# Expert weights loaded as 4 KB runs per partition, and every sixth chunk of them multiplied whole as fp32

## The chip, the core and the metric

The kernel runs on one core of a Trainium2 chip. The metric is device time in microseconds: the span from the first to the last instruction of one execution and the little that lies around it. The median of three executions of the kernel before is 1588.86 us (1588.35 to 1589.14). One execution was recorded by the hardware profiler; it took 1591.64 us, and its span is 1590.0 us. All rows below are from that one.

## The reference, cut to what matters

The reference is one block with a mixer, a memory attention and a hierarchical mixture of experts, and then two more layers with attention and a feed-forward part, on 256 tokens of width 1024 in float32. The change concerns the experts: 32 of them, each with two matrices of 1024 x 512 and one of 512 x 1024.

```python
N_GROUPS = 4
EXPERTS_PER_GROUP = 8
TOPK_IN_GROUP = 2
D_EXPERT = 512

def hier_moe(h, w_rg, b_rg, w_re, b_re, w_gate, w_up, w_down):
    ...
    # one group per token, two experts in it, softmax weights
    def run_block(args):
        e, tok, w = args
        xb = xt[tok]
        hid = jax.nn.silu(xb @ w_gate[e]) * (xb @ w_up[e])
        return (hid @ w_down[e]) * w[:, None].astype(xb.dtype)
```

## The kernel before

All 32 experts are computed, each on up to 32 of its own tokens (tokens beyond that go through a loop that does not run here unless some expert has more than 32). Two experts make a unit; there are 16 units. For each unit, `up(u)` streams 16 chunks of weights (gate and up matrices) and `down(u - 1)` streams 8 chunks of the unit before. So a unit takes 24 chunks, and the stage 384. A chunk is 256 rows of 512 columns of float32, 512 KB: two tiles of 128 x 512 side by side in an SBUF slot (`KC = 2`). `load` (line 276) issues its transfer on SyncE's queue with the row index split as `(k p)`: partition p gets row p of the first 128 rows and row p of the second 128, two runs of 2 KB. For the down matrices the columns are halved and a chunk has 256 rows of one half. `nextraw` hands out the slots in a ring of about 27 places (tiles named raw, kTc, vc, hBl, hAl, hAh, hBh, gain), SyncE issues in order, and each transfer waits until its slot has been read.

A float32 matrix is multiplied in two halves of fp32r, a short type that TensorE multiplies faster. `high` (line 286) makes the high half on ScalarE, `low` (line 291) makes the rest, raw minus high, on VectorE (7 chunks early in the stage on GpSimd). Each has four buffers. `parts` (line 1010) then issues four products of 128 x 512 for the chunk (line 1015): two on the high half, two on the low half. The stationary operand of 128 columns holds both halves of the tokens' rows (32 tokens x 2 experts x high and low), and `comb` adds them later.

`stream` (line 1021) runs over the chunks: it takes the next loaded chunk, has the halves made, issues the products, and then calls `tick`, which runs what was put on an agenda for this number of chunks (`clock`). So small work is placed between the chunks by `at(n, ...)`: copying the gate and up sums (line 1068), adding the halves of the hidden rows (line 1070), the sigmoid and the products that make them (lines 1078 to 1083), copying the down sums Y (line 1099), adding a pair of units to the residual x by products with Y (the scatter, lines 1106 and 1110), and gathering the tokens' rows for the next two units (`take`, line 933, and `put`, lines 940 and 942). Nearly all of it is kept in program order on each engine. `take` multiplies 128 columns of x, taken contiguously, with a 0/1 selection; it gives 128 rows of the transposed x, in the order in which the chunks have their rows.

The scatter and the gather use plain float32 operands; the trace records each such product as two instructions.

Of the kernel before, what the change touches and what calls it, by code (L numbers as in the profile page):

```python
# [13 lines left out]
F32 = mybir.dt.float32  # L14
# [6 lines left out]
P = 128  # L21
# [3 lines left out]
KD = D // P  # L25
KC = 2
RAW = 4
MOE_RAW = 16
LAG = 3
POOLED = (4, 24, 3)  # L30
EARLY = 25
PAST = 16
OVER = 10
# [81 lines left out]
def forward(ctx: ExitStack, tc: tile.TileContext, a: dict, out: bass.AP):  # L115
    nc = tc.nc
    mm = nc.tensor.matmul
# [3 lines left out]
    wraw = ctx.enter_context(tc.tile_pool(name="wraw", bufs=RAW))  # L121
# [10 lines left out]
    def new(pool, shape, dt=F32, name="t", **kw):  # L132
        return pool.tile(shape, dt, name=name, tag=name, **kw)

    def bcast_rows(ap, n=P):

        return bass.AP(tensor=ap.tensor, offset=ap.offset, ap=[[0, n]] + [list(x) for x in ap.ap])
# [75 lines left out]
    def slices(*halves):  # L213

        return [(h[0][:, k], h[1][:, k]) for h in halves for k in range(h[0].shape[1])]
# [53 lines left out]
    def keep(ins):  # L269
        return tc.keep_in_program_order(ins)  # L270

    def chunk(pool, tag, kc, n, dt=F32):
        v = new(pool, [P, KC, 512], dt, name=tag, **({"bufs": 2} if tag == "Y" else {}))
        return v if n == 512 else v.rearrange("p k n -> p (k n)")[:, 0:kc * n].rearrange("p (k n) -> p k n", n=n)

    def load(parts, kc, n, pool=wraw, tag="raw"):

        raw = chunk(pool, tag, kc, n)
        at = 0
        for src in parts:  # L280
            w = src.shape[1]
            nc.sync.dma_start(out=raw[:, :kc, at:at + w], in_=src.rearrange("(k p) n -> p k n", p=P))
            at += w
        return raw

    def high(raw, kc, n, order=free):
        h = chunk(whi, "wh", kc, n, F32R)
        order(nc.scalar.activation(h[:, :kc], raw[:, :kc], AF.Copy))  # L288
        return h

    def low(raw, h, kc, n, order=free, eng=nc.vector):
        l = chunk(wlo, "wl", kc, n, F32R)
        order(eng.tensor_sub(l[:, :kc], raw[:, :kc], h[:, :kc].bitcast(F32)))  # L293
        return l
# [51 lines left out]
    def add_to_x(xs, W, then=None, loaded=None, order=free):  # L346
        for half in range(2):
            hs = slice(half * 512, (half + 1) * 512)

            def evac(t, ps):  # L350
                nc.vector.tensor_add(x[:, t, hs], x[:, t, hs], ps)
                if then:
                    then(x[:, t, hs], t, half)

            dense(xs, [W[:, hs]], 512, evac, 3 if half else 1, loaded if half else None, order)
# [361 lines left out]
    def nextraw():  # L717

        return next(v for v in raws if not closing or v[0] is not big or v[1] in ("kTc", "vc"))

    wg, wu, wd = a["w_exp_gate"][0], a["w_exp_up"][0], a["w_exp_down"][0]
    ahead, ready = collections.deque(), collections.deque()
# [4 lines left out]
    with tc.tile_pool(name="crossp", bufs=1, reuse_waits="tile") as cp:  # L727
# [4 lines left out]
        for h in range(4):  # L732
            ps = new(psm, [P, NT, T], name="mm")
# [6 lines left out]
            p = pair[:, h % 2]  # L740
# [8 lines left out]
        for h in range(4):  # L749
            p = pm[h]  # L750
# [33 lines left out]
        def feed_moe(src, t, half):  # L784
# [19 lines left out]
        xr = new(rowp, [P, NT, D], name="xr")  # L804
# [5 lines left out]
        nc.gpsimd.dma_start(out=rb[:, 4:36], in_=bcast_rows(a["b_router_expert"][0]))  # L810
        first = []
        add_to_x(slices(oT), a["w_co"][0], feed_moe, lambda: first.extend(
            load([wg[0, k0 * P:(k0 + KC) * P, :]], KC, 512, *nextraw()) for k0 in range(0, KD, KC)))
        ss = new(sml, [P, NT], name="s2")
        nc.vector.tensor_add(ss, ssm[:, 0], ssm[:, 1])
        rm = rstd_of(ss, NT, D, "m")
# [16 lines left out]
    def s3(name, n):  # L833
        return new(mp, [P, NT, n], name=name)
# [53 lines left out]
    UNITS = [(2 * u, 2 * u + 1) for u in range(16)]  # L888
    last = len(UNITS) - 1
    xs2 = []  # L890
    for u in range(2):
        xs2.append(new(mp, [P, KD, 3, 2, 32], F32R, name="xs%d" % u))
        if u == 0:
            wt = s3("wt", 32)
            upcoming = [W[e, k0 * P:(k0 + KC) * P] for i in range(2) for e in UNITS[i] for W in (wg, wu) for k0 in range(0, KD, KC)]
            ahead.extend(load([src], KC, 512, *nextraw()) for src in upcoming[len(first):][:EARLY])
    hs2 = []
    for v in xs2:
        nc.gpsimd.memset(v[:, :, 1].bitcast(F32), 0.0)
# [5 lines left out]
    agenda, clock = collections.defaultdict(list), [0]  # L905

    def at(n, fn, *args):
        if n <= 0:
            fn(*args)
        else:  # L910
            agenda[clock[0] + n].append((fn, args))

    def tick():
        clock[0] += 1
        for fn, args in agenda.pop(clock[0], ()):
            fn(*args)
# [11 lines left out]
    def take(u, k0):  # L928

        ps = new(pst, [P, 4, 2, 2, 32], name="tp")  # L930
        for k in range(4):
            for t in range(NT):
                keep(mm(ps[:, k].rearrange("p u e r -> p (u e r)"), xr[:, t, (k0 + k) * P:(k0 + k + 1) * P],
                        sels[u][:, t].rearrange("p e r -> p (e r)"), start=(t == 0), stop=(t == NT - 1)))
        return ps

# [7 lines left out]
    def gather(u, first, step, lag):  # L944
        select(u)
        for i in range(2):
            at(first + step * i, lambda k0: at(lag, put, k0, take(u, k0)), 4 * i)
# [59 lines left out]
        nc.gpsimd.dma_start(out=wodram, in_=wos)  # L1007
        nc.gpsimd.dma_start(out=iddram.rearrange("(o n) -> o n", o=1), in_=ids)

    def parts(xf, e, nk, last, acc, W, col):  # L1010

        def go(k0, ww):
            for i in range(2):
                for k in range(KC):
                    keep(mm(acc, xf[:, k0 + k, e * 64:e * 64 + P], ww[i][:, k],  # L1015
                            start=(e == 0 and k0 == 0 and i == 0 and k == 0),
                            stop=(e == last and k0 + KC == nk and i == 1 and k == KC - 1)))

        return [(W[k0 * P:(k0 + KC) * P, col:col + 512], functools.partial(go, k0)) for k0 in range(0, nk, KC)]

    def stream(chunks):
        for src, go in chunks:
            if ready:
                go(ready.popleft())
            else:
                raw = ahead.popleft() if ahead else load([src], KC, 512, *nextraw())
                h = high(raw, KC, 512, keep)
                go((h, low(raw, h, KC, 512, keep, nc.gpsimd if clock[0] < POOLED[1] and clock[0] % POOLED[0] == POOLED[2] else nc.vector)))
            tick()

    def flat(v):
        return v.rearrange("p k a b c -> p k (a b c)")
# [21 lines left out]

    def up_chunks(u, G=None, U=None):
        return [c for e, x_ in enumerate(UNITS[u]) for acc, W in ((G, wg), (U, wu))
                for c in parts(flat(xs2[u % 2]), e, KD, len(UNITS[u]) - 1, acc, W[x_], 0)]

    def up(u):

# [26 lines left out]
        at(LAG + 2, hidden)  # L1087

    def down_chunks(u, Y=(None, None)):
        return [c for e, x_ in enumerate(UNITS[u]) for half in range(2)  # L1090
                for c in parts(flat(hs2[u % 2]), e, 4, len(UNITS[u]) - 1, Y[half], wd[x_], half * 512)]

    def down(u):

        Y = [new(psa, [P, 512], name="at") for _ in range(2)]
        stream(down_chunks(u, Y))
        Yg[u] = new(mp, [P, 2, 512], name="Y", bufs=2)
        for half in range(2):
            at(LAG - 2 + 2 * half, lambda *v: keep(nc.scalar.copy(*v)), Yg[u][:, half], Y[half])
# [89 lines left out]
    for u in range(last + 1):  # L1189
        if u == last:  # L1190
            closing.append(True)
        if u == last - 1:

            gf, g12 = xr[:, 0], xr[:, 1]
            nc.gpsimd.dma_start(out=gf[0:1], in_=bcast_rows(a["g_final"], 1))
            nc.gpsimd.dma_start(out=g12[0:1], in_=bcast_rows(a["norm_attn_2"][0], 1))
            nc.gpsimd.tensor_tensor(g12[0:1], g12[0:1], gf[0:1], op=ALU.mult)
            for i, (v, half) in enumerate(itertools.product((gf, g12), range(2))):
                at(GAINS + 2 * i, to_all, v[:, half * 512:half * 512 + 512])
        up(u)  # L1200
        if u == OVER:

            for (src, _), v in zip(down_chunks(u - 1) + up_chunks(u + 1), itertools.takewhile(lambda v: v not in shared, raws)):
                ahead.append(load([src], KC, 512, *v))
            overflow()
        if u % 2 and u < last:
            gather(u + 1, 1, 2, 3)
        if u == last:
            sums.extend([new(psm, [P, 512], name="mm") for _ in range(NT)] for _ in range(2))
            for v, n in zip(both, ADDX):  # L1210
                at(n, add, *v, None)
        if u:
            down(u - 1)
            if u % 2 == 0:
                scatter([u - 2, u - 1], LAG + 2, 3, 2)

    Y = [new(psa, [P, 512], name="at") for _ in range(2)]
# [66 lines left out]
    for t, half in both:  # L1284
        v = x[:, t, hs(half)]
# [268 lines left out]
```

## Time and profile before

| | |
|---|---|
| median of three executions | 1588.86 us |
| profiled execution | 1591.64 us, span 1590.0 us |
| mean granted TensorE clock | 0.989 of 2.4 GHz |
| TensorE busy | 1532.9 us, 96% of the span |
| VectorE busy | 1190.1 us, 75% |
| ScalarE busy | 992.1 us, 62% |
| bytes moved | 383.59 MB, 241 GB/s over the span |

A row of the page's groups gives line, engine, operation, the tiles (out<-in), their shapes, the count, the busy time and the mean of one, then the idle time of the engine just before them and what ended it. Busy time of TensorE holds modelled ends of pipelined products, so the distance between starts tells more than a duration. The slices of the page are 1590.0 / 40 = 39.75 us each; the expert products lie in the eighth to the twenty-first.

### The profile page before, as it was taken

What the parts mean: (1) busy time and instruction counts of PE and PEld (TensorE: products, weight loads), DVE (VectorE), ACT (ScalarE), POOL (GpSimd) and SP (SyncE); (2) the same over time, 40 slices, a digit from 0 to 9 for tenths busy, and PEclk for the clock granted to TensorE, in tenths of its full rate; (3) what the DMA queues carried; (4) which work ended last, traced back from release to release, by engine and by line L of the source; (5) the groups of instructions that cost most, each with busy time, mean ns of one, the idle gap of its engine ahead of it and who ended that gap; (6) DMA issues with size and microseconds to landing.
All of it is one profiled execution on the core that took longest, in us unless ns stands there. A gap on an engine that the chain in (4) does not pass through costs nothing. (4 is left out here: it accounts for less than half of the span.)

```text
span 1590.0 us, 20604 instructions
## 1 busy us (share of the span) xinstructions
PE 1532.9 (96%) x7099; PEld 1194.5 (75%) x7099; DVE 1190.1 (75%) x1498; ACT 992.1 (62%) x1353; POOL 199.8 (13%) x95
## 2 busy tenths in 40 slices
PE   7999999699999999999999999999999999999998
PEld 5778887466776767767667887888888887888886
DVE  5665575789999999999887876766656876766654
ACT  5455554579878887797774666555544566455543
POOL 1110000434335141142001000000000000000000
PEclk9999999899999999999999999999999999999999
DMA  8645559689999999999956545566567545566653
GB/s 283 218 137 160 182 173 375 209 295 370 386 387 387 386 387 340 341 386 386 387 187 195 147 141 164 182 189 186 185 186 220 168 137 152 178 195 186 184 187 106
DMA packets 220348, 383.59 MB, mean 241 GB/s; under 512 B 13464, under 2 KB 60000, under 8 KB 219856
## 3 DMA queue, kind: packets, MB, share of 16 engines
q1 hardware_dynamic: 217584, 373.76, 70.2%
q0 software_dynamic: 1648, 6.84, 1.4%
q10 hardware_dynamic: 1008, 1.64, 0.3%
q8 instruction: 57, 0.93, 0.2%
q14 instruction: 51, 0.42, 0.1%
HBM read 381.10 MB, written 2.65 MB: 241 GB/s over the span
## 5 line engine op out<-in xcount | busy, mean ns | idle before, releaser
L293 DVE TENSOR_TENSOR wl<-raw,wh 128x1024 fp32r<-128x1024 f32 x599 | 718.0, 1227 | 239.6 <-ACT wh L288 226.1
L288 ACT ACTIVATE wh<-raw 128x1024 fp32r<-128x1024 f32 x606 | 624.0, 1057 | 303.2 <-PE mm L327 258.9
L1015 PE MATMUL mm<-wl,xs 128*128 128x512 f32 x512 | 186.4, 446 | 8.6 <-DVE wl L293 5.5
L1039 POOL TENSOR_TENSOR selw<-sel,wt 128x128 f32<-128x128 f32 x32 | 139.7, 4385 | 272.9 <-DVE sel L925 187.6
L1015 PE MATMUL mm<-wh,xs 128*128 128x512 f32 x512 | 164.0, 403 | 0.6 <-ACT wh L288 0.6
L1015 PEld LDWEIGHTS mm<-wl,xs 128*128 128x128 f32 x512 | 91.3, 192 | 66.2 <-DVE wl L293 32.8
L327 PE MATMUL mm<-wh,hAl 128*128 128x512 f32 x424 | 139.1, 409 | 0.0
L327 PE MATMUL mm<-wh,hAh 128*128 128x512 f32 x424 | 134.3, 397 | 2.7 <-ACT wh L288 2.7
L327 PE MATMUL mm<-wl,hAh 128*128 128x512 f32 x424 | 134.3, 398 | 0.0
L327 PE MATMUL mm<-wl,hBh 128*128 128x512 f32 x424 | 133.3, 394 | 0.0
L327 PE MATMUL mm<-wh,hBl 128*128 128x512 f32 x424 | 132.4, 393 | 0.1
L327 PE MATMUL mm<-wh,hBh 128*128 128x512 f32 x424 | 132.1, 393 | 0.0
L1015 PEld LDWEIGHTS mm<-wh,xs 128*128 128x128 f32 x512 | 97.0, 191 | 27.2 <-ACT wh L288 3.7
L1015 PE MATMUL at<-wl,hs 128*128 128x512 f32 x256 | 89.4, 430 | 7.9 <-DVE wl L293 7.9
L327 PEld LDWEIGHTS mm<-wh,hAh 128*128 128x128 f32 x424 | 79.3, 190 | 19.8 <-ACT wh L288 3.1
L1015 PE MATMUL at<-wh,hs 128*128 128x512 f32 x256 | 87.2, 422 | 5.4 <-ACT wh L288 5.3
L327 PEld LDWEIGHTS mm<-wl,hAh 128*128 128x128 f32 x424 | 79.4, 190 | 17.2
L327 PEld LDWEIGHTS mm<-wh,hBh 128*128 128x128 f32 x424 | 78.9, 188 | 17.6
L327 PEld LDWEIGHTS mm<-wh,hBl 128*128 128x128 f32 x424 | 78.5, 188 | 18.0 <-issue 1.4
L327 PEld LDWEIGHTS mm<-wl,hBh 128*128 128x128 f32 x424 | 78.5, 188 | 16.9 <-issue 0.3
L327 PEld LDWEIGHTS mm<-wh,hAl 128*128 128x128 f32 x424 | 75.3, 191 | 12.3 <-issue 0.8
L1015 PEld LDWEIGHTS at<-wl,hs 128*128 128x128 f32 x256 | 45.1, 188 | 34.9 <-DVE wl L293 21.9
(482 smaller groups left out, 2245.5 us busy)
## 6 DMA issues: line engine op xcount, KB each, us to landing
raw<-in_w_in_dram SPq DMA_DIRECT2D x121, 512.0 KB, 3.7
raw<-in_w_exp_down_dram SPq DMA_DIRECT2D x101, 512.0 KB, 10.8
raw<-in_w_exp_gate_dram SPq DMA_DIRECT2D x95, 512.0 KB, 10.8
raw<-in_w_exp_up_dram SPq DMA_DIRECT2D x93, 512.0 KB, 10.8
raw<-in_w_ffn_in_dram SPq DMA_DIRECT2D x176, 256.0 KB, 3.2
raw<-in_w_ffn_out_dram SPq DMA_DIRECT2D x44, 512.0 KB, 3.8
raw<-in_w_out_dram SPq DMA_DIRECT2D x24, 512.0 KB, 3.8
raw<-in_w_ckv_dram SPq DMA_DIRECT2D x8, 512.0 KB, 3.9
```

Of the source, the lines that this page charges most:

```text
L288: order(nc.scalar.activation(h[:, :kc], raw[:, :kc], AF.Copy))
L293: order(eng.tensor_sub(l[:, :kc], raw[:, :kc], h[:, :kc].bitcast(F32)))
L327: order(mm(ps[t][:, :n], xs[k0 + k][part][:, t * P:(t + 1) * P], ww[:, k, :n], start=(k0 == 0 and i == 0 and k == 0), stop=(k0 + kc == nk ...
L1015: keep(mm(acc, xf[:, k0 + k, e * 64:e * 64 + P], ww[i][:, k], start=(e == 0 and k0 == 0 and i == 0 and k == 0), stop=(e == last and k0 + K ...
L1039: nc.gpsimd.tensor_tensor(selw[:, :, :, d], sel, wt[:, :, 2 * u:2 * u + 2].rearrange("p t (e o) -> p t e o", o=1).to_broadcast([P, NT, 2, ...
```

## The change

`load_rows` loads an expert chunk with the row index split as `(p k)`: partition p gets rows 2p and 2p + 1, which stand next to each other in memory, as one run of 4 KB. For the down matrices of all units but the last a chunk is now 128 whole rows of 1024 columns, also 4 KB a partition, and its products go to both halves of Y in turn. The gather takes the columns of x with a step of two, so that its rows have the same order as the weights. And in `stream`, a chunk whose number gives 4 when divided by 6, beyond number 24, gets no halves: its raw tile is multiplied as float32, two products of 128 x 512 with the same token rows read as float32. These are the numbers 28, 34, ... 382, 60 chunks. The eight chunks of the last unit's down matrices keep the old layout.

```diff
+WHOLE = (6, 4)
...
+    def load_rows(src, pool=wraw, tag="raw"):
+
+
+        rows, n = src.shape
+        raw = new(pool, [P, KC, 512], name=tag, **({"bufs": 2} if tag == "Y" else {}))
+        nc.sync.dma_start(out=raw.rearrange("p k n -> p (k n)"), in_=src.rearrange("(p k) n -> p (k n)", p=P))
+        return raw
...
-            load([wg[0, k0 * P:(k0 + KC) * P, :]], KC, 512, *nextraw()) for k0 in range(0, KD, KC)))
+            load_rows(wg[0, k0 * P:(k0 + KC) * P, :], *nextraw()) for k0 in range(0, KD, KC)))
...
-            ahead.extend(load([src], KC, 512, *nextraw()) for src in upcoming[len(first):][:EARLY])
+            ahead.extend(load_rows(src, *nextraw()) for src in upcoming[len(first):][:EARLY])
...
-                keep(mm(ps[:, k].rearrange("p u e r -> p (u e r)"), xr[:, t, (k0 + k) * P:(k0 + k + 1) * P],
+                first = (k0 + k) // KC * KC * P + k % KC
+                keep(mm(ps[:, k].rearrange("p u e r -> p (u e r)"), xr[:, t, first:first + KC * (P - 1) + 1:KC],
                         sels[u][:, t].rearrange("p e r -> p (e r)"), start=(t == 0), stop=(t == NT - 1)))
...
-    def parts(xf, e, nk, last, acc, W, col):
+    def fetch(src, place):
+        return load(src, KC, 512, *place) if isinstance(src, list) else load_rows(src, *place)
+
+    def parts(xf, e, nk, last, acc, W, col=None):
+
+
+        kc = KC // len(acc)
 
         def go(k0, ww):
-            for i in range(2):
-                for k in range(KC):
-                    keep(mm(acc, xf[:, k0 + k, e * 64:e * 64 + P], ww[i][:, k],
-                            start=(e == 0 and k0 == 0 and i == 0 and k == 0),
-                            stop=(e == last and k0 + KC == nk and i == 1 and k == KC - 1)))
-
-        return [(W[k0 * P:(k0 + KC) * P, col:col + 512], functools.partial(go, k0)) for k0 in range(0, nk, KC)]
+            for i, w in enumerate(ww):
+                rows = xf if len(ww) == 2 else xf.bitcast(F32)
+                for k in range(kc):
+                    for j, v in enumerate(acc):
+                        keep(mm(v, rows[:, k0 + k, e * 64:e * 64 + P], w[:, k * len(acc) + j],
+                                start=(e == 0 and k0 == 0 and i == 0 and k == 0),
+                                stop=(e == last and k0 + kc == nk and i == len(ww) - 1 and k == kc - 1)))
+
+        at = [slice(k0 * P, (k0 + kc) * P) for k0 in range(0, nk, kc)]
+        return [(W[v] if col is None else [W[v, col:col + 512]], functools.partial(go, v.start // P)) for v in at]
...
-                raw = ahead.popleft() if ahead else load([src], KC, 512, *nextraw())
-                h = high(raw, KC, 512, keep)
-                go((h, low(raw, h, KC, 512, keep, nc.gpsimd if clock[0] < POOLED[1] and clock[0] % POOLED[0] == POOLED[2] else nc.vector)))
+                raw = ahead.popleft() if ahead else fetch(src, nextraw())
+                if clock[0] % WHOLE[0] == WHOLE[1] and clock[0] > POOLED[1]:
+
+                    go((raw,))
+                else:
+                    h = high(raw, KC, 512, keep)
+                    go((h, low(raw, h, KC, 512, keep, nc.gpsimd if clock[0] < POOLED[1] and clock[0] % POOLED[0] == POOLED[2] else nc.vector)))
...
     def down_chunks(u, Y=(None, None)):
-        return [c for e, x_ in enumerate(UNITS[u]) for half in range(2)
-                for c in parts(flat(hs2[u % 2]), e, 4, len(UNITS[u]) - 1, Y[half], wd[x_], half * 512)]
+        es = list(enumerate(UNITS[u]))
+        hf = flat(hs2[u % 2])
+        if u < last:
+            return [c for e, x_ in es for c in parts(hf, e, 4, len(es) - 1, Y, wd[x_])]
+
+        return [c for e, x_ in es for half in range(2) for c in parts(hf, e, 4, len(es) - 1, Y[half:half + 1], wd[x_], half * 512)]
```

## Rows read from the trace of the kernel before

**Rows 1.** The page: traffic in 40 equal slices of the span, GB/s.

```profile
GB/s 283 218 137 160 182 173 375 209 295 370 386 387 387 386 387 340 341 386 386 387 187 195 147 141 164 182 189 186 185 186 220 168 137 152 178 195 186 184 187 106
```

**Rows 2.** Order of time (start, duration): chunks' issue and use; issues: landing.

```profile
440.31 0.45 SPq L282 DMA_DIRECT2D hAl<-in_w_exp_down_dram  x1
470.55 1.05 ACT L288 ACTIVATE wh<-hAl 128x1024 fp32r<-128x1024 f32 x1
704.43 0.75 SPq L282 DMA_DIRECT2D hBl<-in_w_exp_up_dram  x1
720.99 1.06 ACT L288 ACTIVATE wh<-hBl 128x1024 fp32r<-128x1024 f32 x1
raw<-in_w_exp_up_dram SPq DMA_DIRECT2D x93, 512.0 KB, 10.8
```

**Rows 3.** Waits from 370 to 600 us (total, times, longest), SyncE's queue last.

```profile
PEld mm L1015 <- DVE wl L293: 11.7, 33, 0.4
SPq L282 <- DVE wl L293: 49.0, 80, 2.6
```

**Rows 4.** ScalarE in order of time: copies of Y two units apart.

```profile
453.91 0.57 ACT L1099 COPY Y<-at 128x512 f32<-128x512 f32 x1
517.84 0.57 ACT L1099 COPY Y<-at 128x512 f32<-128x512 f32 x1
```

**Rows 5.** Instruction groups from 453.91 to 517.84 us, one pair of units.

```profile
L293 DVE TENSOR_TENSOR wl<-raw,wh 128x1024 fp32r<-128x1024 f32 x36 | 41.6, 1217 | 0.7 <-ACT wh L288 0.7
L288 ACT ACTIVATE wh<-raw 128x1024 fp32r<-128x1024 f32 x36 | 35.7, 1055 | 1.2 <-PE mm L1015 1.2
L1106 PE MATMUL tp<-Y,selT 128*128 128x512 f32 x16 | 8.2, 591 | 0.0
L1070 PE MATMUL mm<-c_ones,rows 128*128 128x64 f32 x32 | 4.0, 268 | 0.0
L933 PE MATMUL tp<-sel,xr 128*128 128x128 f32 x32 | 3.9, 277 | 0.0
```

**Rows 6.** VectorE in order of time: start, duration of all, count.

```profile
441.84 4.62 DVE L293 TENSOR_TENSOR wl<-raw,wh 128x1024 fp32r<-128x1024 f32 x4
```

**Rows 7.** Stretches: busy of PE, PEld, DVE, ACT, POOL; clock, DMA, GB/s.

```profile
453.91:517.84 63.93, 61.92 (x278) 45.34 (x277) 61.35 (x64) 53.51 (x68) 24.43 (x4) 1.00 1.05 386
743.00:826.00 83.00, 79.23 (x305) 54.41 (x306) 74.35 (x69) 64.33 (x78) 5.35 (x3) 0.98 0.85 310
```

**Rows 8.** TensorE in order of time: scatter, split products, hidden rows, gather.

```profile
452.26 1.02 PE L1106 MATMUL tp<-Y,selT 128*128 128x512 f32 x2
453.58 0.63 PE L1015 MATMUL mm<-wh,xs 128*128 128x512 f32 x2
454.05 0.63 PE L1015 MATMUL mm<-wl,xs 128*128 128x512 f32 x2
...
478.62 1.00 PE L1070 MATMUL mm<-c_ones,rows 128*128 128x64 f32 x8
479.46 2.00 PE L933 MATMUL tp<-sel,xr 128*128 128x128 f32 x16
481.22 0.72 PE L1015 MATMUL at<-wh,hs 128*128 128x512 f32 x2
```

**Rows 9.** ScalarE and TensorE in order of time behind the hidden rows.

```profile
446.09 0.39 ACT L1078 ACTIVATE hid<-mm 128x256 f32<-128x256 f32 x1 [1.99 <-PE mm L1070]
448.83 0.73 PE L1015 MATMUL at<-wh,hs 128*128 128x512 f32 x2 [0.88 <-ACT wh L288]
450.09 0.73 PE L1015 MATMUL at<-wl,hs 128*128 128x512 f32 x2 [0.52 <-DVE wl L293]
485.46 0.72 PE L1015 MATMUL at<-wl,hs 128*128 128x512 f32 x2 [0.60 <-DVE wl L293]
```

**Rows 10.** SyncE issues a gain vector; the stretch of highest traffic after it.

```profile
24.59 0.42 SPq L183 DMA_DIRECT2D gain<-in_g_mem_dram  x1
28.00:29.00 1.00, 0.76 (x3) 0.43 (x4) 0.21 (x2) 0.07 (x1) 0.00 (x0) 1.00 1.05 424
```

More of the change, by code (lines that the diff above doesn't have):

```diff
@@ L1056, in up_chunks @@
         return [c for e, x_ in enumerate(UNITS[u]) for acc, W in ((G, wg), (U, wu))
-                for c in parts(flat(xs2[u % 2]), e, KD, len(UNITS[u]) - 1, acc, W[x_], 0)]
+                for c in parts(flat(xs2[u % 2]), e, KD, len(UNITS[u]) - 1, [acc], W[x_])]
     def up(u):
@@ L1203, in forward @@
             for (src, _), v in zip(down_chunks(u - 1) + up_chunks(u + 1), itertools.takewhile(lambda v: v not in shared, raws)):
-                ahead.append(load([src], KC, 512, *v))
+                ahead.append(load_rows(src, *v))
             overflow()
```

## The prediction

> **What bounds the kernel now.** I read the page first for busy shares by slice, then the expert stage alone: table of stretches, waits by engine, instruction groups of one pair of units, and last the order of time on TensorE, VectorE, ScalarE and SyncE. The change touches only the stage of expert products, about 297 to 826 us, 384 chunks of 512 KB. The page shows 386 to 387 GB/s there in most slices [rows 1], and over two units TensorE is busy 61.92 and VectorE 61.35 of 63.93 us [rows 7]: three resources look full. Three readings separate them.
>
> First, the transfers. SyncE issues chunk hAl at 440.31 us; a chunk of this stage lands 10.8 us after issue (the median), so at 451.1, and ScalarE takes it at 470.55: a lead of 19.4 us. It is the same for hBl, issued at 704.43 and taken at 720.99, with 5.8 us [rows 2]; I followed all 384 chunks in this way, in their order, and this lead is the shortest. No compute engine waits for a transfer; the longest waits of PE's loads are for VectorE's low halves, and SyncE itself waits for VectorE to free a slot [rows 3]. The transfers keep up, no more.
>
> Second, VectorE. Two units (48 chunks) take 63.9 us, from one copy of Y to the copy two units later [rows 4]. VectorE makes 48 low halves in it; the row shows the 36 of raw [rows 5], 12 lie under other names of slots. Four back to back take 4.62 us [rows 6]: with a last one of 1.217, three steps of 1.135 each. 48 x 1.135 = 54.5; with its 16 smaller operations it is busy 61.35 of 63.9 [rows 7], and what is left is a wait inside the chain told below: it sets the pace today.
>
> Third, TensorE. Its busy 61.92 [rows 7] holds waiting inside modelled ends, so I count starts. A pair of split products steps by 0.47 us (453.58 to 454.05; 0.466 over a longer run of them), so a chunk of four takes 0.932. A full fp32 product of the same 128x512 shape also exists before: the scatter of Y. It starts at 452.26; the two split products drawn in behind it and it together give way to the next at 453.58: 1.32 - 0.466 = 0.854 us for one fp32 product, recorded as two instructions [rows 8]. Per pair [rows 5, 8]: 48 x 0.932 = 44.7; 16 records of the scatter are 8 products, 6.8; 32 of the gather at 1.76 per 16, 3.5; 32 of the hidden rows at 0.84 per 8, 3.4; the rest under 0.5. Sum 58.5 of 63.9, so TensorE truly idles 5.4 us a pair.
>
> **The change, part by part.** *Whole chunks.* Places 28, 34, ... 382 of the 384 are multiplied whole: 60 chunks, 8 a pair. Each drops one high half on ScalarE (1.055 us each) [rows 5] and one low half on VectorE; VectorE's pair falls from 61.35 by 8 x 1.135 to 52.3, and the engine stops being the limit. TensorE gets two fp32 products for four split ones: 2 x 0.854 - 0.932 = +0.78 us, 60 times, +47 us in all. Per pair 58.5 + 6.2 = 64.8 us: more than the 63.9 the pair takes now, before any idle. TensorE is what comes last next.
>
> How much of the 5.4 us of idle remains? The part that is VectorE's pace (some 2.9, gaps too short for the view) goes. The part at the hidden rows stays: ScalarE's sigmoid waits for TensorE (446.09), two VectorE products, a cast and the next high half follow, and TensorE waits 0.88 and 0.52 us in one unit and 0.60 in the other [rows 9]. 28 mod 24 is 4 and a unit has 24 chunks, so whole chunks fall on the same places of each unit, the 3rd of the eight down chunks among them; none lies in the two chunks that cover this chain, so it stays, at some 3 us a pair with the small waits that follow it (VectorE needs 1.135 a chunk there, TensorE 0.932, and only a whole chunk lets it catch up). *Down order.* Both halves of Y now end with the last down chunk; before, half 0 ended two chunks sooner. ScalarE's copy of half 0 stands one step behind the last chunk and will wait for TensorE; behind it queue the next high halves, and TensorE waits for those. The nearest row is the same kind of wait, 0.88 [rows 9]; bounds 0 and 1 us a unit; I take 0.5, 1 us a pair, since the next chunk is a whole one and covers part. So 4 us of idle, 68.8 us a pair, +4.9; 356 chunks from place 28 on are 7.4 pairs: +36.
>
> Where TensorE has more to spare this is softened: from 743 to 826 us it is busy 79.23 of 83.0 at a granted clock of 0.98, VectorE 74.35 [rows 7], with single gaps behind slow VectorE operations that the relief should close. I take off 6. Sum: **+30 us**.
>
> *4 KB runs.* At 387 GB/s a chunk takes 1.355 us. A gain vector broadcast in rows of 4 KB is issued at 24.59 us behind half of mem, also in rows of 4 KB; the best microsecond behind them moved 424 GB/s [rows 10], which would be 1.24 us a chunk. With a lead of 5.8 to 20 us this gains nothing: the consumer comes last. The cost is nothing too unless the rate falls below 48 x 0.524 MB / 68.8 us = 366 GB/s, from where it would bind. A whole chunk's slot is freed by TensorE and not by VectorE, some chunks later; SyncE waits in order for it, and the same lead hides that. If the lead is gone, each late slot costs what it is late, 1 to 4 us.
>
> The Trainium skill (Perfetto Trace Analysis, DMA Optimizations) says that going from 2 KB to 4 KB transfers can raise throughput much when a kernel is bound by its DMA. Here the row of the lead says it is not; by the rule alone 384 x (1.355 - 1.24) = 44 us would go.
>
> *Gather.* The rows of x that a chunk needs are now taken with a step of two elements as the stationary operand, 128 loads per half as before. No stepped load stands in the trace. It reads no fewer elements, so no gain; at most twice the 0.110 us a record takes now [rows 8], so another 0.110 on each of the gather's 256 records, +28 us. I take 0, by the contiguous row. By the Trainium skill (SBUF - State Buffer, Door 1) a step of up to four fp32 elements stays within one 16-byte line and is free; the sum by it is the same, and no run here shows it yet.
>
> **The rivals.**
> *TensorE soaks it up.* All idle of a pair goes: 64.8 - 63.9 = 0.9 x 7.4 = +7, 1596 us. For it: VectorE gains 9 and ScalarE 8 us a pair of slack. Against: the chain at the hidden rows is latency, not load.
> *Nothing gained on idle, or a stepped load that costs.* 64.8 + 5.4 gives +6.3 x 7.4 = +47, 1636; with +28 for the gather on top of my sum, 1647.
> *Faster.* One mechanism: an fp32 product of a raw tile costs less than the scatter's. It decides from 0.55 us a product (58.5 - 8 x 0.932 + 16 x 0.55 + 4.0 = 63.9). At 0.466 the pair is 62.5, -1.4 x 7.4, 1578 us; at 0.233 TensorE falls to 54.8 and the transfers come last, 48 x 1.24 = 59.4, -33, 1556 us. Against: [rows 8] has the same shape and type at 0.854. This is also the only way in which the 4 KB runs could show.
>
> **How the numbers follow.** The profiled execution took 1591.64 us (span 1590.0), the median of three is 1588.86, 2.8 less. 1591.6 + 30 - 2.8 = 1619 us. Chances: the forecast with +15 to +45, 0.62; soaked up, +3 to +15, 0.13; beyond +45, 0.10; within 0.2% (3.2 us, about what a measurement of this kernel can tell from no change), 0.05; faster, 0.10. The range from 1592 to 1645 leaves out the faster cases, most of no change and the far end of a dear gather.
>
> **What would show it.** Right: fp32 products on raw at 0.85 us each; a pair of units at 67 to 70 us; VectorE near 52 us busy per pair; PE waits at the hidden rows and at high halves behind Y's copy; the chunks land earlier before use and GB/s in the stage falls below 386. Wrong: the pair below 63.9, or TensorE waiting for transfers, or the gather's 16 records taking 3 us and not 1.76. The forecast falls if the fp32 product on raw is under 0.55 us.

## The result, and the profile after

| | before | after |
|---|---|---|
| median | 1588.83 us | 1624.84 us (1623.95 to 1625.03) |
| ratio, with its 95% interval | | 1.0231 (1.0218 to 1.0244) |
| profiled execution, span | 1591.64, 1590.0 us | 1625.03, 1623.4 us |
| a pair of units (48 chunks) | 63.93 us | 69.54 us |

The change makes the kernel 36.0 us slower; 30 were forecast. The page of after, first its busy times and then traffic in its 40 slices (each 1623.4 / 40 = 40.6 us):

```profile
PE 1568.2 (97%) x7099; PEld 1194.8 (74%) x7099; DVE 1130.5 (70%) x1438; ACT 938.0 (58%) x1293; POOL 97.9 (6%) x95
...
GB/s 282 220 134 163 190 184 355 239 295 398 340 388 346 349 385 307 285 409 409 298 206 166 164 145 153 170 198 187 186 184 214 178 143 144 181 194 182 183 191 107
```

The flat run of 386 and 387 of [rows 1] is gone. Most slices of the stage are lower, since the consumer asks for less, but in two the queue runs at 409, a rate that no slice before reaches: the longer runs do move more when they are let.

The copies of Y in order of time on ScalarE, as in [rows 4] (start, duration, and in brackets the idle time before and its releaser):

```profile
458.62 0.58 ACT L1126 COPY Y<-at 128x512 f32<-128x512 f32 x1 [2.22 <-PE at L1033]
...
528.16 0.58 ACT L1126 COPY Y<-at 128x512 f32<-128x512 f32 x1 [2.23 <-PE at L1033]
```

A pair takes 528.16 - 458.62 = 69.54 us. The bracket is new: ScalarE stands still for 2.2 us until the last down chunk is through TensorE. The stretch between them, busy times in the columns of [rows 7], and groups of it as in [rows 5]:

```profile
458.62:528.16 69.54, 67.51 (x277) 46.15 (x276) 53.84 (x55) 46.23 (x58) 5.40 (x4) 1.00 0.94 361
...
L302 DVE TENSOR_TENSOR wl<-raw,wh 128x1024 fp32r<-128x1024 f32 x30 | 35.4, 1229 | 5.1 <-ACT wh L297 4.5 <-DMA hAh<-in_w_exp_down_dram 0.5
L297 ACT ACTIVATE wh<-raw 128x1024 fp32r<-128x1024 f32 x30 | 29.9, 1058 | 2.2 <-PE mm L1033 2.2
L1033 PE MATMUL mm<-raw,xs 128*128 128x512 f32 x20 | 9.4, 592 | 0.0
L943 PE MATMUL tp<-sel,xr 128*128 128x128 f32 x32 | 4.1, 283 | 0.0
```

VectorE fell from 61.35 to 53.84 us (7.5 less, where 9.1 were forecast) and ScalarE from 53.51 to 46.23; TensorE rose from 61.92 to 67.51. VectorE is no longer near the length of the pair. The fp32 products on raw are the new group (20 records here, 12 more under other names of slots: 32 records, 16 products, 8 chunks). The 0.5 us that VectorE's group puts down to a transfer is no wait for its chunk: the slot named is not the one that it reads.

TensorE in order of time, one whole chunk and its neighbours, then the second gather of the pair, as in [rows 8]:

```profile
466.69 0.63 PE L1033 MATMUL mm<-wl,xs 128*128 128x512 f32 x2
467.15 1.88 PE L1033 MATMUL mm<-raw,xs 128*128 128x512 f32 x4
468.47 1.03 PE L1033 MATMUL mm<-wh,xs 128*128 128x512 f32 x2
469.34 0.63 PE L1033 MATMUL mm<-wl,xs 128*128 128x512 f32 x2
...
488.67 2.10 PE L943 MATMUL tp<-sel,xr 128*128 128x128 f32 x16
490.53 0.71 PE L1033 MATMUL at<-wh,hs 128*128 128x512 f32 x2
...
493.44 0.63 PE L1033 MATMUL at<-wh,hs 128*128 128x512 f32 x2
494.67 0.73 PE L1033 MATMUL at<-wl,hs 128*128 128x512 f32 x2 [0.60 <-DVE wl L302]
495.25 0.63 PE L1033 MATMUL at<-wh,hs 128*128 128x512 f32 x2
...
522.60 0.63 PE L1033 MATMUL at<-wl,hs 128*128 128x512 f32 x2
524.09 0.73 PE L1033 MATMUL at<-wh,hs 128*128 128x512 f32 x2 [0.87 <-ACT wh L297]
525.35 0.73 PE L1033 MATMUL at<-wl,hs 128*128 128x512 f32 x2 [0.53 <-DVE wl L302]
525.92 0.63 PE L1033 MATMUL at<-wh,hs 128*128 128x512 f32 x2
```

From 467.15 to 469.34 stand two fp32 products and one pair of split ones (0.466 us): (2.19 - 0.466) / 2 = 0.86 us a product. The last seven lines are the chain at the hidden rows: 0.60, 0.87 and 0.53 us in the brackets, the same waits as 0.60, 0.88 and 0.52 in [rows 9]. The starts show that a wait costs more than its bracket says: from 493.44 on the steps are 1.23 and 0.58 us, from 522.60 on 1.49, 1.26 and 0.57, where two split products back to back take 0.466. That is 5.13 - 5 x 0.466 = 2.8 us in all, against 2.0 in the brackets.

Waits from 370 to 600 us, as in [rows 3]:

```profile
DVE wl L302 <- ACT wh L297: 28.9, 26, 2.2
ACT Y L1126 <- PE at L1033: 15.9, 7, 2.3
PEld mm L1033 <- DVE wl L302: 4.6, 15, 0.5
...
SPq L292 <- DVE wl L302: 99.9, 96, 4.4
SPq L292 <- PE mm L1033: 39.1, 19, 5.5
```

The waits of PE's loads for low halves fell from 11.7 to 4.6 us, and VectorE now waits for ScalarE. SyncE waits longer for slots than before (49.0 us for VectorE then), which is the transfers having more time than they need. The shortest leads of split chunks, the first of the stage aside, are about 8 us (7.8 the shortest of all). One of them is the chunk in slot gain, issued and used so (SyncE, then ScalarE, in order of time):

```profile
662.73 0.43 SPq L292 DMA_DIRECT2D gain<-in_w_exp_up_dram  x1
...
681.38 1.04 ACT L297 ACTIVATE wh<-gain 128x1024 fp32r<-128x1024 f32 x1
```

That is 18.7 us from issue to use, of which 10.5 are the transfer in a busy stretch. Over most of the stage the lead is 15 to 33 us.

### The profile page after: what moved, and what is told of

The parts are those of the page before. It is cut to its first block, busy times and chain, and to the rows that moved or that the text cites. A ratio compares the mean times of both kernels' runs of the same rounds, so it can differ in the third digit from the quotient of the medians.

```text
span 1623.4 us, 20375 instructions
## 1 busy us (share of the span) xinstructions
PE 1568.2 (97%) x7099; PEld 1194.8 (74%) x7099; DVE 1130.5 (70%) x1438; ACT 938.0 (58%) x1293; POOL 97.9 (6%) x95
## 5 line engine op out<-in xcount | busy, mean ns | idle before, releaser
L302 DVE TENSOR_TENSOR wl<-raw,wh 128x1024 fp32r<-128x1024 f32 x556 | 674.2, 1232 | 285.8 <-ACT wh L297 268.9
L297 ACT ACTIVATE wh<-raw 128x1024 fp32r<-128x1024 f32 x563 | 582.7, 1058 | 306.8 <-PE mm L336 258.0
L1033 PE MATMUL mm<-wl,xs 128*128 128x512 f32 x426 | 151.2, 436 | 10.0 <-DVE wl L302 5.6
L1033 PE MATMUL mm<-wh,xs 128*128 128x512 f32 x426 | 151.7, 438 | 0.6 <-ACT wh L297 0.6
L1033 PEld LDWEIGHTS mm<-wl,xs 128*128 128x128 f32 x426 | 77.5, 188 | 53.1 <-DVE wl L302 22.1
L1033 PEld LDWEIGHTS mm<-wh,xs 128*128 128x128 f32 x426 | 79.1, 189 | 42.2 <-issue 18.0
L1033 PE MATMUL at<-wh,hs 128*128 128x512 f32 x222 | 77.2, 429 | 4.4 <-ACT wh L297 4.4
L1033 PE MATMUL at<-wl,hs 128*128 128x512 f32 x222 | 73.7, 413 | 7.4 <-DVE wl L302 7.4
L1062 POOL TENSOR_TENSOR selw<-sel,wt 128x128 f32<-128x128 f32 x32 | 38.5, 1221 | 401.6 <-DVE sel L934 294.7
L1033 PEld LDWEIGHTS at<-wl,hs 128*128 128x128 f32 x222 | 38.2, 188 | 29.3 <-DVE wl L302 23.5
```

The costliest lines, as they stand in the source:

```text
L1033: keep(mm(v, rows[:, k0 + k, e * 64:e * 64 + P], w[:, k * len(acc) + j], start=(e == 0 and k0 == 0 and i == 0 and k == 0), stop=(e == last ...
L1062: nc.gpsimd.tensor_tensor(selw[:, :, :, d], sel, wt[:, :, 2 * u:2 * u + 2].rearrange("p t (e o) -> p t e o", o=1).to_broadcast([P, NT, 2, ...
```

## Experiments

All are compared with the kernel before on the same chip, 1587.6 to 1587.8 us. The changed kernel (called after below) was measured on another occasion, beside 1588.83, so a difference of 2 or 3 us between it and a run is hardly one. The first four take the change apart.

**The 4 KB runs alone.** The changed kernel with no whole chunk.

```diff
-WHOLE = (6, 4)
+WHOLE = (6, 6)
```

> The changed kernel with no whole chunk: 4 KB loads, down chunks of whole rows and the stepped gather stay, all 384 chunks are split again. If TensorE's longer products cost the 36 us: 1584 to 1594 us, a pair of units at 63 to 64.5. Rival, the new layout costs (stepped gather, late copies of Y, loads): 1600 us or more, a pair over 65.5.

Measured: 1604.57 us, ratio 1.0098 (1.0075 to 1.0122). The layout of the loads, with the new order of the down chunks and of the gather, costs 17 us where I expected about nothing. The stretch of a pair, in the columns above, and where ScalarE stands in it:

```profile
457.08:523.56 66.48, 64.47 (x278) 44.70 (x277) 61.82 (x64) 53.48 (x67) 5.79 (x4) 1.00 0.98 381
...
454.69 0.59 ACT L1126 COPY Y<-at 128x512 f32<-128x512 f32 x1 [1.27 <-PE at L1033]
...
490.25 0.59 ACT L1126 COPY Y<-at 128x512 f32<-128x512 f32 x1 [1.41 <-PE at L1033]
```

A pair is 66.48 us with VectorE's work unchanged (61.82 against 61.35). ScalarE waits 1.3 to 1.4 us in each unit at the copy of Y, which before had no wait in [rows 4].

**Whole chunks alone.** The kernel before, its 2 KB loads and its order of down chunks, with the fp32 branch.

```diff
-                h = high(raw, KC, 512, keep)
-                go((h, low(raw, h, ...)))
+                if clock[0] % WHOLE[0] == WHOLE[1] and clock[0] > POOLED[1]:
+                    go((raw,))
+                else:
+                    h = high(raw, KC, 512, keep)
+                    go((h, low(raw, h, ...)))
...
```

> The kernel before with every sixth chunk multiplied whole and nothing else: 2 KB loads, halves of down columns, contiguous gather. If TensorE's longer products cost the 36 us: 1618 to 1627 us, a pair near 69. Rival, the layout costs: under 1605 us. If the late copies of Y cost the 1 us a pair that was put on them, it is 7 us below the changed kernel.

Measured: 1615.04 us, 1.0172 (1.015 to 1.0193), a pair 68.43 us. The time lies between the two forecasts, nearer the first. So the whole chunks cost 27 us by themselves, and the 4 KB runs add 10 to them, less than the 17 that they cost alone.

```profile
455.40:523.83 68.43, 66.56 (x277) 46.30 (x276) 53.77 (x56) 46.47 (x58) 3.44 (x4) 1.00 1.02 366
```

**The relief without the price.** The changed kernel, in which every sixth chunk uses its high half twice.

```diff
-                    go((raw,))
+                    h = high(raw, KC, 512, keep)
+                    go((h, h))
```

> The changed kernel, but every sixth chunk keeps its four short products and only its low half is not made: the high half is used twice, so the low part of these 60 chunks is left out of the result. It gives VectorE its relief of 9 us a pair without any price on TensorE. If VectorE sets the pace before, with TensorE idle 5.4 us a pair: the pair falls to TensorE's 58.5 plus 4 of idle, 62.5, 1578 us, or to the transfers' 61.5 at best, 1571. Rival, TensorE with waits of its own already sets the pace: 63.5 to 64, 1586 to 1590.

Measured: 1592.1 us, 1.0024 (1.0012 to 1.0036). VectorE is relieved (53.65 us a pair) and the time stays at that of before: a pair takes 64.5 us, with ScalarE waiting for Y as in the first experiment. I had expected 1571 to 1578; the rival came nearer. The kernel to set beside it is that of the 4 KB runs alone, with the same layout and nothing taken from VectorE: 1604.57 us. So the relief is worth 12.5 us here, where TensorE has the short products.

**The price without the relief.** The changed kernel, in which the halves of a whole chunk are made and thrown away.

```diff
+                    low(raw, high(raw, KC, 512, keep), KC, 512, keep)
                     go((raw,))
```

> The changed kernel, but the whole chunks still have both halves made on ScalarE and VectorE, unused: TensorE's price without any relief. If TensorE comes last in the changed kernel and VectorE has 17 us a pair to spare there: 1624 to 1632 us, a pair near 69.6 to 70.5, hardly above the changed kernel. Rival, the relief gives back a good part of the price: 1640 us or more.

Measured: 1627.6 us, 1.0253 (1.023 to 1.0275), 2.8 us above after (whose interval, 1.0218 to 1.0244, overlaps with this one). VectorE does its old work (62.63 us) and it hardly matters.

```profile
458.90:528.65 69.75, 67.71 (x278) 45.90 (x277) 62.63 (x64) 53.95 (x68) 5.39 (x4) 1.00 0.97 362
```

With the whole chunks in place the relief is worth about 3 us, not 12.5, and the price is about 33 (after less the relief alone), or 23 without any relief (this run less the 4 KB runs alone). A relief pays where the relieved engine comes last: TensorE comes last in the changed kernel.

**Was VectorE really the pace before?** The kernel before, with the high half used twice in every sixth chunk.

```diff
-                go((h, low(raw, h, ...)))
+                if clock[0] % 6 == 4 and clock[0] > POOLED[1]:
+                    go((h, h))
+                else:
+                    go((h, low(raw, h, ...)))
```

> The kernel before, where every sixth chunk has no low half and uses its high half twice (the low part of 60 chunks is left out of the result): VectorE's relief with no price and no new layout. If VectorE sets the pace before: 62 to 62.7 us a pair, and since 48 chunks of 2 KB runs need 65.0 us of transfers the lead is eaten by the end: 1576 to 1584 us. Rival, TensorE's own waits set it: 63.4 or more a pair, 1585 us or more.

Measured: 1580.76 us, 0.9954 (0.9937 to 0.9971), a gain of 7 us. VectorE did set the pace, but by little. The stretch of a pair, and TensorE's waits in it with the products around them:

```profile
447.26:509.59 62.33, 60.32 (x277) 46.11 (x276) 53.53 (x56) 53.30 (x67) 4.23 (x4) 1.00 1.05 386
...
479.83 0.63 PE L1015 MATMUL at<-wh,hs 128*128 128x512 f32 x2
481.06 0.73 PE L1015 MATMUL at<-wl,hs 128*128 128x512 f32 x2 [0.60 <-DVE wl L293]
481.63 0.63 PE L1015 MATMUL at<-wh,hs 128*128 128x512 f32 x2
...
505.39 0.62 PE L1015 MATMUL at<-wl,hs 128*128 128x512 f32 x2
506.90 0.73 PE L1015 MATMUL at<-wh,hs 128*128 128x512 f32 x2 [0.88 <-ACT wh L288]
508.16 0.73 PE L1015 MATMUL at<-wl,hs 128*128 128x512 f32 x2 [0.53 <-DVE wl L293]
508.73 0.63 PE L1015 MATMUL at<-wh,hs 128*128 128x512 f32 x2
```

Take 7.8 us of low halves from VectorE, and the pair gives back 1.6, while the waits of the chain at the hidden rows stay: 2.0 us in the brackets, 2.8 by the starts (1.23 + 0.57 + 1.51 + 1.26 + 0.57 - 5 x 0.466). Where the 1.6 lay can be read in the kernel before. In a run of chunks ahead of the hidden rows TensorE goes at VectorE's step:

```profile
496.82 0.73 PE L1015 MATMUL mm<-wl,xs 128*128 128x512 f32 x2
...
504.76 0.74 PE L1015 MATMUL mm<-wl,xs 128*128 128x512 f32 x2
```

Seven chunks lie between these two starts, 1.134 us each and not 0.932: 1.4 us of the 1.6. The view shows no wait there, because the modelled ends of the products cover it.

**The late copies of Y.** The next two put the copies of Y two chunks later, so that ScalarE doesn't reach them before TensorE has finished; first in the changed kernel, then in the 4 KB runs alone. The edit of both:

```diff
-            at(LAG - 2 + 2 * half, lambda *v: keep(nc.scalar.copy(*v)), Yg[u][:, half], Y[half])
+            at(LAG - 2 + 2 * half + 2 * (u < last - 1), lambda *v: keep(nc.scalar.copy(*v)), Yg[u][:, half], Y[half])
```

> The changed kernel with the two copies of Y put two chunks later (all units but the last two), so that ScalarE does not reach them before TensorE has ended the down chunks. A pair is 69.5 us in the changed kernel and 68.4 with whole chunks alone. If the late copies cost the 1.1: 68.4 to 68.8, 1616 to 1619 us. Rival, the stepped gather or the loads cost it: 69.5 and 1623 to 1627 us as it is.

Measured: 1614.69 us, 1.0174 (1.0152 to 1.0197), 10 us below after and level with the whole chunks alone. But the pair of units that stands above for after takes 69.08 us here (455.07 to 524.15), only 0.46 less and above the 68.4 to 68.8 of the forecast; over 7.4 pairs that is 3.4 us, not 10. The trace shows where most of the rest comes from. Two other pairs of this run (from 387.71 and from 662.12 us) take 67.36 us, where the pairs of after take 69.55. In both the scatter's products, which are not kept in program order (their `mm` has no `keep`), now stand where TensorE waits for the chain at the hidden rows, and two of its three waits are gone (0.86 and 0.53 us in the brackets, 1.7 by the starts). So it looks in the first of them:

```profile
449.97 1.88 PE L1133 MATMUL tp<-Y,selT 128*128 128x512 f32 x4
451.29 1.03 PE L1033 MATMUL at<-wh,hs 128*128 128x512 f32 x2
```

So this run holds two effects, the copies and a moved scatter, and no run separates them.

> The kernel of runs alone (no whole chunk) with the same two copies two chunks later. Runs alone take 66.5 us a pair, 2.6 above the kernel before, and ScalarE waits 2.7 us a pair for the end of the down chunks. If that wait is the cost: 63.9 to 64.3 a pair, 1586 to 1591 us. Rival, stepped gather or loads: 66 or more, 1600 us or more.

Measured: 1593.07 us, 1.0034 (1.0018 to 1.0049). The time lies between the two forecasts: of the 17 us of the 4 KB runs alone 11.5 were the late copies, and about 5 remain. Here the stretch agrees, 64.49 us a pair and not 66.48, and VectorE is idle for 2.62 us of it and not 4.66. ScalarE's wait at the copy is 0.33 us in the changed kernel with this edit (2.22 without), and gone in the 4 KB runs alone:

```profile
524.15 0.59 ACT L1126 COPY Y<-at 128x512 f32<-128x512 f32 x1 [0.33 <-PE at L1033]
```

The stretch of a pair in the 4 KB runs with later copies:

```profile
449.59:514.08 64.49, 62.49 (x278) 45.46 (x277) 61.87 (x65) 53.95 (x68) 7.28 (x4) 1.00 0.99 389
```

**The stepped gather.** Two runs ask whether it is the rest of 5 us: the step alone in the kernel before, and the kernel just above with contiguous columns again.

```diff
-                keep(mm(ps[:, k].rearrange("p u e r -> p (u e r)"), xr[:, t, (k0 + k) * P:(k0 + k + 1) * P],
+                first = (k0 + k) // KC * KC * P + k % KC
+                keep(mm(ps[:, k].rearrange("p u e r -> p (u e r)"), xr[:, t, first:first + KC * (P - 1) + 1:KC],
```

> The kernel before with one edit: the gather takes the columns of x with a step of two. The weights keep their old layout, so each chunk is multiplied with other columns of x than its own; the amount of work is the same. It measures the stepped gather by itself. In the changed kernel 16 records took 1.79 and 1.86 us where before took 1.70 and 1.76. Theory (the step costs about 6% of each record and nothing else): 16 records take 1.8 us, 0.2 us a pair of units, and the time is 1588 to 1590. Rival (the stepped gather is what remained of the cost of the 4 KB runs when the copies of Y were put back): 1592 to 1594.

Measured: 1589.76 us, 1.0008 (0.9998 to 1.0017), and 16 records take 479.20 - 477.35 = 1.85 us (1.76 in [rows 8]):

```profile
477.35 2.10 PE L934 MATMUL tp<-sel,xr 128*128 128x128 f32 x16
479.20 0.71 PE L1016 MATMUL at<-wh,hs 128*128 128x512 f32 x2
```

> The 4 KB runs with no whole chunk and Y copied two chunks later, as before, with the gather taking contiguous columns again. The weights keep the 4 KB layout, so each chunk is multiplied with other columns of x than its own; the amount of work is the same. With the stepped gather this took 1593.07, 5 us over the kernel before. Theory (the step costs little, the rest is the transfers and slots): 1591 to 1593. Rival (the step is the rest): 1588 to 1590. If both this and the step alone show nothing, the 5 us stand open.

Measured: 1594.35 us, 1.0038 (1.0023 to 1.0052), the same as with the step. So the gather isn't the rest. A pair took 0.5 us longer than before in both of these (64.49 with the step, 64.39 without), with VectorE as much longer busy. The trace shows where most of that lies. Two products of GpSimd (selw) fall beside four low halves of VectorE (GpSimd, then VectorE, in the run with the step):

```profile
484.45 2.26 POOL L1062 TENSOR_TENSOR selw<-sel,wt 128x128 f32<-128x128 f32 x2 [9.92 <-PE mm L1069]
...
483.89 5.04 DVE L302 TENSOR_TENSOR wl<-raw,wh 128x1024 fp32r<-128x1024 f32 x4
```

These four take 5.04 us where four take 4.62 in [rows 6]: 0.42 of the 0.5 us. It is so in each of the five pairs of both runs. In four of the five pairs of the kernel before the product that GpSimd starts at this place lasts 19.0 us, and no low half beside it is longer. No run moved these products, so this is read from the traces and not shown by an experiment, and why it comes out differently in the two layouts stays open.

**Where the whole chunks stand.** Two runs place a whole chunk beside the chain at the hidden rows: the 4 KB runs with the later copies and just one whole chunk a unit, and the changed kernel with the later copies and all its whole chunks moved.

```diff
-WHOLE = (6, 6)
+WHOLE = (24, 12)
```

> Runs with later copies of Y, and one whole chunk in each unit of 24, the one that TensorE has beside the hidden rows' chain on ScalarE and VectorE (number 12 of 24), where TensorE waits 0.8 to 1.7 us. Price 0.78 us a unit, relief 1.135 us on VectorE, and the wait shrinks by up to 0.8 and more. If the price lies in a wait: 62.8 to 63.9 a pair, 1580 to 1588 us, at or below the kernel before. Rival, the price adds anywhere: 65.5, 1598 us.

Measured: 1596.04 us, 1.0055 (1.004 to 1.0071), in time nearer the rival, a pair 64.48 us against 64.49 without them. Two whole chunks a pair cost 2 x 0.78 us on TensorE, and the waits of 0.60 and 0.88 us at the chain went; only one is left:

```profile
512.21 0.73 PE L1033 MATMUL at<-wl,hs 128*128 128x512 f32 x2 [0.53 <-DVE wl L302]
```

By the starts those two waits had cost 0.87 and 1.03 us. The whole chunks, 1.56 us dearer together, fill them, and nothing is gained.

```diff
-WHOLE = (6, 4)
+WHOLE = (6, 0)
```

> The changed kernel with Y copied two chunks later and the whole chunks moved: numbers that give 0 when divided by 6 (30, 36, ... 378, 59 of them), so that one of them in each unit lies beside the chain at the hidden rows, where one such chunk a unit had closed most of TensorE's single waits. With the old places this took 1614.69 and a pair of 69.1 us. Theory of the prediction (about 3 us of the idle of a pair is the chain at the hidden rows, and a whole chunk there covers it): a pair of 66 to 67 us and 1592 to 1601. Rival (what idle is left is spread over the pair and has little to do with that chain): a pair of 68.5 to 69.5 and 1610 to 1616.

Measured: 1611.33 us, 1.0145 (1.0128 to 1.0162): the time is in the rival's range, the pair between the two forecasts. A pair fell from 69.08 to 67.48 us, 1.6 of the 1.9 that the two covered waits cost by the starts (0.60 and 0.86 in the brackets); the third stayed, with no whole chunk beside it. Of the 7.6 us by which the stage ended sooner in the profiled executions (its last copy of Y at 847.07 and not 854.66 us) half was lost again behind it (spans 1613.7 and 1609.9). The one wait left, and the stretch:

```profile
518.21 0.73 PE L1033 MATMUL at<-wl,hs 128*128 128x512 f32 x2 [0.52 <-DVE wl L302]
...
455.93:523.41 67.48, 66.88 (x278) 46.42 (x276) 53.72 (x56) 46.21 (x59) 4.86 (x4) 1.00 0.97 379
```

None of the kernels that compute every product beat the kernel before.

## Why the prediction was right

**Which resource comes last: right.** VectorE before: taking its work away alone gives 7 us. TensorE after: giving VectorE its work back costs about 3 us. The transfers are last in neither.

**The fp32 product: right, 0.86 us for 0.854.** The scatter of [rows 8] was the row to take. The rival that decided from 0.55 us was far off.

**The idle that stays: near, by terms that were wrong both ways.** I counted 58.5 us of TensorE work a pair before by the starts, so 5.4 idle, and let 4.0 stay: 3 at the hidden rows and 1 at Y. (The 2.9 us that I gave to VectorE's pace do not fit beside the 3: together they are 5.9, not 5.4.) The 3 at the hidden rows was right. Read by the starts, as the 58.5 was, the three waits of the chain cost 2.8 us in both kernels, and the next chunk at VectorE's step another 0.2. VectorE's pace was 1.6 (63.93 - 62.33). The 0.8 left of the 5.4 I let go without a row, and it stayed: small products that the count had at almost nothing (selw), and first products behind another kind, 0.55 us for two in place of 0.466 (481.22 in [rows 8] to 481.77), at five to eight places of a pair of units. After's pair then is 58.5 + 6.2 + 3.0 + 0.8, 0.2 for the gather, 0.46 for the copies of Y and 0.4 for two more chunks at VectorE's step behind the chain: 69.6. 69.54 was measured, 68.8 forecast. The 0.7 that it fell short is 0.8 + 0.2 + 0.4 left out, less the 0.5 too much for Y and 0.1 of rounding (58.5 + 6.2 is 64.7, not 64.8); x 7.4 that is the 5 to 6 us by which 30 fell short of 36. The way and the rough size follow from the mechanism; that the sum came so near is in part luck, as these errors work against each other.

**Late copies of Y: right in kind, twice too large here.** I took 1 us a pair, 7 in all; the pair shown gives back 0.46 when the copies move. The mechanism (ScalarE in order, the next high halves behind the copy) shows as the 2.2 us in the bracket. The 10 us that moving the copies gave in all come in part from the scatter that moved with them. What I did not see is that alone, without whole chunks, the same copies cost 2.0 us a pair and 11.5 in all: ScalarE waits 1.3 us there and VectorE, already the pace, then waits for it.

**The last stretch: near in size, only in part where I put it.** A pair is 5.6 us longer; x 7.4 is 41, and 36.0 were measured (36.7 at the end of the stage in the profiled executions, the last copy of Y at 826.53 and 863.25 us), so 5 came off where I took 6. Only about 2 of them lie behind 743 us, in the stretch that I had named.

**4 KB runs gain nothing: right.** The lead was there before and grew. The ceiling did rise, 387 to 409 GB/s (424 was my row), and nobody was waiting for it. By the rule of the Trainium skill (Perfetto Trace Analysis, DMA Optimizations) larger transfers pay when the DMA bounds the kernel. The runs agree with its condition: here nothing waited for the DMA, and the 44 us did not come. That the layout itself would cost 5 us, besides Y, was not in the prediction.

**The gather: taken at 0, measured at 0 to 3 us.** The Trainium skill (SBUF — State Buffer, Door 1) counts a step of up to four fp32 elements as free. Here a step of two made 16 records take 1.85 instead of 1.76 us, 5% more, so for these records the measurement differs from the page; on the whole kernel the interval is -0.3 to +2.7 us.

**Rivals.** "TensorE soaks it up" fell: the chain's waits stand in after to a hundredth as before. "Nothing gained on idle" (1636) fell on the other side: the 1.6 us of VectorE's pace did go, though about 0.9 came back at the copies of Y and behind the chain.

## What to carry to other kernels

Before work is moved from the engine that sets the pace to another, ask how far behind that other engine is: here VectorE led TensorE by 1.6 us a pair, so a relief of 9 us could return 1.6, and a price of 6 us on TensorE was paid nearly whole. What such a relief is worth depends on who comes last then: 7 and 12.5 us in the two layouts with TensorE's short products, about 3 with the long ones. Measure an engine's work and its waits in the same way: the three waits of the chain cost 2.8 us by the starts and 2.0 by the brackets, because the ends of products are modelled. Work that has to be done anyway covers such a wait, as the scatter did; a whole chunk put there only pays for itself. When the order of chunks is changed, move the work that is placed by counting chunks too, or an engine that runs in order stops at it.

## What the hardware showed that I had not expected

Runs of 4 KB a partition moved 409 GB/s in whole slices where runs of 2 KB stopped at 387, 6% more. A stationary operand read with a step of two fp32 elements made 16 gather records take 1.85 instead of 1.76 us.

The same small GpSimd product can take 0.4 or 19.0 us, and low halves of VectorE beside it can be longer too. In the pair of the kernel before that [rows 5] shows, the third of the four products lasts 19.0 us (the fourth 0.4), while VectorE makes one low half after the other without a longer one among them:

```profile
491.61 19.40 POOL L1039 TENSOR_TENSOR selw<-sel,wt 128x128 f32<-128x128 f32 x2 [13.24 <-PE mm L1046]
```

In the 4 KB runs with later copies the same two products take 2.26 us (the line at 484.45 above), and two low halves beside them take 1.43 and 1.42 us where others take 1.22. VectorE is about as busy in both stretches, 61.35 and 61.87 us, so its load alone does not decide it. Whether the two engines hold each other up, and what decides which of them loses, was not tried.
